# A pointwise convolution's weight folded into the lower half of an output projection, on one Trainium2 core

## The chip, the cores and the metric

The kernel runs on 1 core of one Trainium2 chip. The metric is the device time of one execution in microseconds (us), as the median of several runs. The engines are called as the profile calls them: PE is TensorE's matmul, PEld its weight load, DVE is VectorE, ACT is ScalarE, POOL is GpSimd, SP is SyncE, which here only issues DMAs. SPq and ACTq are the DMA queues of SP and ACT.

## What is computed

One decoder layer for 2048 tokens and a model width of 1024, in float32. Cut to what matters:

```python
def conformer_conv(u, conv_dw, conv_dw_b, conv_ln_g, conv_ln_b, w_conv_pw):
    a, gate = jnp.split(u, 2, axis=-1)
    h = a * jax.nn.sigmoid(gate)
    h = causal_depthwise_conv(h, conv_dw) + conv_dw_b          # 31 taps
    h = jax.nn.silu(layer_norm(h, conv_ln_g, conv_ln_b))
    return h @ w_conv_pw                                       # 512 x 512

...
        hn = rms_norm(h, mix_pre_g)
        proj = hn @ w_in                                       # 1024 x 1792
        attn_out = sliding_window_attention(q, k, v, attn_sinks, rel_bias)
        conv_out = conformer_conv(u, ...)
        mixed = jnp.concatenate([attn_out, conv_out], axis=-1) @ w_out   # 1024 x 1024
        h = h + rms_norm(mixed, mix_post_g)
        hn = rms_norm(h, ffn_pre_g)
        ff = (jax.nn.silu(hn @ w_gate) * (hn @ w_up)) @ w_down
        h = h + rms_norm(ff, ffn_post_g)
```

The convolution's part of the mixed output is swish(...) @ w_conv_pw @ w_out[512:1024]: two matrix products in a row with nothing between them.

## The kernel before

The 2048 tokens are worked in four tiles of 512 (NT = 4, T = 512), the 1024 channels in eight blocks of 128 (KC = 8). Float32 products are made from two parts: each operand is split into a rounded high part and the low rest, and `three` (L165) issues high x high, high x low and low x high into one PSUM bank. A split is one copy on ACT for the high part and one subtraction on POOL or DVE for the low part (`split_w`, L106, for weights). Low parts that are used again are kept in DRAM (`lo_in`, `lo_out`), so that later tiles load them.

The stages, by the letter that stands after @ in the profile's tile names (fc@C is a tile fc that stage C made; the names that the profile prints leave the tile's number out):

- A, t = 0 to 3: the input projection, 14 units of 24 matmuls of 128x128 by 512 columns each. Weights pass through `raw` (2 buffers) and `w` (6 buffers).
- B: sliding window attention in blocks of 128 tokens, with its bands and transposes in PSUM tiles tr.
- C: the convolution. `stage_taps` (L536) runs the 31 taps on DVE and keeps the result in DRAM (y_scr). `stage_tail` (L550) transposes it, takes the layer norm, transposes back, forms the swish in `conv_tail` (L565) and multiplies by w_conv_pw. That last part, per tile: four splits of the swish, then for each of four output blocks a load of a weight block (w_pw), a split, 4 x 3 = 12 matmuls into the PSUM tile ct, a copy z by ACT with a factor of one half, and a store to `mixT` on ACT's queue. So 48 matmuls in each of four tails.
- W, w = 0 to 3: the output projection (`stage_w`, L670). It loads the activations from mixT (blocks 0 to 3 attention, 4 to 7 convolution) and splits them, takes w_out in pairs of blocks and halves of the columns through `weight` (L117), and adds the partial sums on DVE. W0 splits the weights itself and stores the low parts to `lo_out`; W1 to W3 split the high part again and load the low part.
- H: transposes and operands for the feed-forward. F and G: its up and down products, in two halves of two tiles (0, 1 and 2, 3), by a scheme with seven instead of eight products.

What sets the order: one generator per stage yields between pieces of work with an estimate of the TensorE time that they take. `run` (L1309) drives a main generator (A, then W1, F, F, G, and again), and after each of its yields pumps the lanes: lists of side stages, each with a rate, the share of the main work's time that its own may use (class Lane, L1234). Tails C0 and C1 are in lane ld; C2, W2, C3, W3 follow each other in lane lw beside the first G. Taps are in lane lc, with a lower priority on DVE. W0 starts when the fourth projection tile has started and C0 is done (L1321). From these emissions a scheduler makes one fixed order for each engine; each engine and each DMA queue then works strictly in that order.

Buffers that are named below: wx has 1, mid 4, chl 5, mb 2, fc 3, w 6, raw 2, the PSUM banks mm 4, tr 3, ct 1.

## Time and profile before

| | us |
|---|---|
| median of 3 runs | 2050.37 |
| lowest and highest run | 2043.07, 2054.49 |
| span of the profiled execution | 2045.2 |

The page gives no other time for the profiled execution than its span, from the first to the last instruction. A row of a group reads: line, engine, operation, tile written <- tiles read, shapes, count | busy us, mean ns of one | idle time of the engine just before them and what ended it. A row of the timeline begins with its start and its length in us. A row of a stretch (window) gives for each engine its busy time and in brackets its count, then the clock granted to TensorE as a share of full speed, the DMA engines' busy share and GB/s. A row of waits reads: engine and line, what was waited for, us in total, how often, the longest. A DMA row gives the queue, the count, the size of one and the median us from issue to landing.

Where the stages lie in the span, by the first and last matmuls of the timeline: W0 and the fourth projection tile from about 338 to 487 us, W1 and the operands H to about 610, the first G from 1036 to 1393. The products of the four tails stand at 290.7 to 330, 497.6 to 536, 1120 to 1150 and in the stretch up to 1295.

### The profile page before, as it was taken

Reading aid. Unit: us, or ns where it says so; the run is one execution under the profiler, and the core shown is the slowest. Engines: PE = TensorE matmul, PEld = TensorE weight load, DVE = VectorE, ACT = ScalarE, POOL = GpSimd, SP = SyncE. Lnnn points to the kernel's source line nnn. Section 1 sums busy time; section 2 is a strip of 40 time slices with the busy share of each in tenths; the row PEclk is TensorE's granted clock in tenths of the full one; section 3 lists DMA queues with packets and bytes.
Section 4 is the critical chain, followed back from the end, with each engine's and each line's share of the span. In section 5 each row is a group of like instructions: output and inputs, shape, how many; then the busy total and the mean of one; then the engine's idle time right before and its main releaser. Section 6 shows DMA issues by size and latency. Waiting matters only on the chain. (4 is left out here: it accounts for less than half of the span.)

```text
span 2045.2 us, 27190 instructions
## 1 busy us (share of the span) xinstructions
PE 1959.9 (96%) x8826; PEld 1565.3 (77%) x8826; DVE 1499.2 (73%) x2623; ACT 984.4 (48%) x1938; POOL 408.5 (20%) x466
## 2 busy tenths in 40 slices
PE   8999999999989999999989999999999999999997
PEld 6777767776667778778878878877788888888886
DVE  4999896995885899887749985577666665545557
ACT  5355455456546633334346457556643433345443
POOL 4011223333111300000001012115423333221003
PEclk9999999999999999999999999999999999999998
DMA  8787645578559876884486778678954453366654
GB/s 305 256 300 228 205 135 185 180 235 279 186 155 330 292 242 224 294 270 168 140 262 205 231 260 287 191 278 304 337 177 162 149 169 112 103 236 212 206 190 144
DMA packets 235902, 451.44 MB, mean 221 GB/s; under 512 B 23496, under 2 KB 49264, under 8 KB 235760
## 3 DMA queue, kind: packets, MB, share of 16 engines
q1 hardware_dynamic: 215216, 419.30, 62.6%
q10 hardware_dynamic: 20544, 30.42, 4.0%
q8 instruction: 69, 1.13, 0.2%
q14 instruction: 73, 0.60, 0.1%
HBM read 330.60 MB, written 119.02 MB: 220 GB/s over the span
## 5 line engine op out<-in xcount | busy, mean ns | idle before, releaser
L85 DVE SCALAR_TENSOR_TENSOR fc@C<-glu@C,colt,fc@C 128x512 f32<-128x512 f32 x480 | 367.7, 778 | 3.5
L846 PE MATMUL mm@F<-hl@H,w@F 128*128 128x512 f32 x1056 | 253.3, 390 | 2.5 <-ACT mm@F L886 1.5
L1116 PE MATMUL mm@G<-hl@G,hl@G 128*128 128x512 f32 x924 | 230.0, 398 | 8.2 <-DVE x@G L85 4.8
L846 PEld LDWEIGHTS mm@F<-hl@H,w@F 128*128 128x128 f32 x1056 | 197.6, 188 | 44.7 <-ACT mm@F L886 2.3
L170 PE MATMUL mm@A<-hl@A,w@A 128*128 128x512 f32 x840 | 207.3, 398 | 5.2 <-ACT w@A L110 1.4
L1116 PEld LDWEIGHTS mm@G<-hl@G,hl@G 128*128 128x128 f32 x924 | 174.6, 191 | 47.0 <-ACT hl@G L759 6.9
L1116 PE MATMUL mm@G<-w@G,hl@G 128*128 128x512 f32 x876 | 199.4, 389 | 0.0
L759 ACT ACTIVATE w@F<-chl@F 128x512 fp32r<-128x512 f32 x220 | 134.8, 624 | 130.9 <-PE mm@F L846 122.2
L1116 PEld LDWEIGHTS mm@G<-w@G,hl@G 128*128 128x128 f32 x876 | 164.4, 188 | 34.1
L170 PEld LDWEIGHTS mm@A<-hl@A,w@A 128*128 128x128 f32 x840 | 155.9, 189 | 42.2 <-ACT w@A L110 2.2
L85 DVE TENSOR_TENSOR w@F<-chl@F,w@F 128x512 fp32r<-128x512 f32 x198 | 145.4, 738 | 33.8 <-ACT w@F L759 33.4
L846 PE MATMUL mm@F<-ql@H,w@F 128*128 128x512 f32 x528 | 127.9, 391 | 11.0 <-ACT w@F L759 7.3
L846 PE MATMUL mm@F<-mid@H,w@F 128*128 128x512 f32 x528 | 130.4, 392 | 2.8 <-ACT mm@F L886 2.6
L846 PE MATMUL mm@F<-p@H,w@F 128*128 128x512 f32 x528 | 130.6, 393 | 0.0
L846 PE MATMUL mm@F<-x@H,w@F 128*128 128x512 f32 x528 | 127.4, 395 | 2.3 <-ACT fa@F L908 2.3
L846 PEld LDWEIGHTS mm@F<-ql@H,w@F 128*128 128x128 f32 x528 | 98.6, 188 | 33.7 <-ACT w@F L759 8.1
L846 PEld LDWEIGHTS mm@F<-x@H,w@F 128*128 128x128 f32 x528 | 99.8, 190 | 24.0 <-ACT fa@F L908 2.8
L846 PEld LDWEIGHTS mm@F<-mid@H,w@F 128*128 128x128 f32 x528 | 98.3, 188 | 26.0 <-ACT mm@F L886 4.6
L846 PEld LDWEIGHTS mm@F<-p@H,w@F 128*128 128x128 f32 x528 | 100.1, 190 | 21.3 <-ACT at@F L1007 0.4
L170 PE MATMUL mm@W<-w@W,hl@W 128*128 128x512 f32 x384 | 102.3, 411 | 7.7 <-ACT hl@W L681 6.8
L110 ACT ACTIVATE w@A<-raw@A 128x512 fp32r<-128x512 f32 x110 | 67.6, 627 | 82.7 <-PE mm@A L170 50.8
L476 POOL TENSOR_SCALAR_AFFINE_SELECT p@B<-p@B 128x512 f32<-128x512 f32 x62 | 59.1, 959 | 228.0 <-ACT p@B L474 226.3
(301 smaller groups left out, 3422.8 us busy)
## 6 DMA issues: line engine op xcount, KB each, us to landing
mids<-fa@F SPq DMA_DIRECT2D x154, 256.0 KB, 2.8
raw@A<-w_in SPq DMA_DIRECT2D x55, 512.0 KB, 4.5
w@A<-lo_in SPq DMA_DIRECT2D x84, 256.0 KB, 3.5
fc@G<-mids SPq DMA_DIRECT2D x77, 256.0 KB, 3.5
fa@G<-mids SPq DMA_DIRECT2D x75, 256.0 KB, 4.3
gb@F<-keeps SPq DMA_DIRECT2D x72, 256.0 KB, 4.3
raw@W<-w_out SPq DMA_DIRECT2D x32, 512.0 KB, 5.1
w@W<-lo_out SPq DMA_DIRECT2D x48, 256.0 KB, 3.9
```

The lines of the kernel that those rows point to most:

```text
L85: r = op(*args, **kw)
L110: act(w[:, 0], raw, AF.Copy)
L170: mat(o, a, b, start=first and i == 0, stop=last and i == n - 1)
L476: nc.gpsimd.affine_select(out=pg[:, kb].rearrange("p (i q) -> p i q", q=P), in_=pg[:, 1].rearrange("p (i q) -> p i q", q=P), compare_op=AL ...
L759: act(w[:, 0], x, AF.Copy)
L846: mat(o, w[:, a, ks], op[k][:, b], start=first and n == 0, stop=n == 11, skip_group_check=not first)
L1116: mat(banks[b], p_, q_, start=start and z == 0, stop=stop and z == 2, skip_group_check=True)
```

## The change

w_conv_pw and the lower half of w_out are multiplied once, by a new stage U (`stage_fold`), to a 512 x 1024 matrix. It is split into high and low parts and kept in DRAM (`fold`). The convolution's tail stops at the swish and stores that to mixT, with the factor of one half moved into the constants lnh. W's lower half loads both parts from `fold` in one DMA of 512 KB per block and splits nothing there. The stores to mixT go through SP's queue instead of ACT's. w_conv_pw is passed to the kernel transposed.

```diff
-    lo_out = dr.tile([2, KC, P, T], F32, name="lo_out")
+    lo_out = dr.tile([2, KC // 2, P, T], F32, name="lo_out")
+    fold = dr.tile([2, 4, P, 2, T], F32, name="fold")
...
             v = f2("fc")
-            act(v, b, AF.Identity, scale=ln_g[:, c : c + 1], bias=ln_b[:, c : c + 1])
+            act(v, b, AF.Identity, scale=lnh[:, c : c + 1], bias=lnh[:, 4 + c : 5 + c])
             stt(v, th, 1.0, v, ALU.add, ALU.mult)
-            h = hl("chl")
-            act(h[:, 0], v, AF.Copy)
-            ptt(h[:, 1], v, h[:, 0].bitcast(F32), ALU.subtract)
-            sc.append(h)
-            yield 2
-            lab[0] = L
-        for m in range(4):
-            raw = f2("fc")
-            nc.sync.dma_start(raw, w_pw[m])
-            w = split_w(raw, "mb" if t == 1 and m % 2 else "chl").rearrange("p a (k c) -> p a k c", c=P)
-            o = ct()
-            three(o, [((w[:, 0, k], w[:, 1, k]), (sc[k][:, 0], sc[k][:, 1])) for k in range(4)])
-            z = f2("gb" if t > 1 else "fc")
-            act(z, o, AF.Copy, scale=0.5)
-            nc.scalar.dma_start(mixT[4 + m, :, t * T : (t + 1) * T], z)
-            yield 2
-            lab[0] = L
+            nc.sync.dma_start(mixT[4 + c, :, t * T : (t + 1) * T], v)
+            yield YZ
+            lab[0] = L
+
+    def stage_fold():
+        lab[0] = "U0"
+
+        def two(src):
+            raw = f4("wx", (P, 2, T))
+            nc.sync.dma_start(raw, src)
+            return raw
+
+        wp = []
+        for i in range(2):
+            lab[0] = "U0"
+            raw = two(w_pw[2 * i : 2 * i + 2].rearrange("c p t -> p c t"))
+            wp += [split_w(raw[:, j], "mid") for j in range(2)]
+            yield 2.76
+        for n in range(2):
+            wo = []
+            for i in range(2):
+                lab[0] = "U0"
+                c = 4 + 2 * i
+                raw = two(w_out[c : c + 2, :, n * T : (n + 1) * T].rearrange("c p t -> p c t"))
+                wo += [split_w(raw[:, j], "chl") for j in range(2)]
+                yield 0.1 if n else 2.76
+            for m in range(4):
+                lab[0] = "U0"
+                o = mm()
+                ms = slice(m * P, (m + 1) * P)
+                three(o, [((wp[j][:, 0, ms], wp[j][:, 1, ms]), (wo[j][:, 0], wo[j][:, 1])) for j in range(4)])
+                f = hl("chl" if m % 2 else "mb")
+                act(f[:, 0], o, AF.Copy)
+                vtt(f[:, 1], o, f[:, 0].bitcast(F32), ALU.subtract)
+                nc.sync.dma_start(fold[n, m], f.bitcast(F32))
+                yield 2.76
...
-                ws = weight(w_out[2 * gi : 2 * gi + 2, :, n * T : (n + 1) * T].rearrange("c p t -> p c t"),
-                            lo_out[n, 2 * gi : 2 * gi + 2], w > 0)
+                if G * gi < 4:
+                    ws = weight(w_out[2 * gi : 2 * gi + 2, :, n * T : (n + 1) * T].rearrange("c p t -> p c t"),
+                                lo_out[n, 2 * gi : 2 * gi + 2], w > 0)
+                else:
+                    ws = [hl("w") for _ in range(2)]
+                    for j in range(2):
+                        nc.sync.dma_start(ws[j].bitcast(F32), fold[n, 2 * gi - 4 + j])
...
+    YZ = 1.0
...
+    lu = Lane(0.6, 0)
...
-    lanes = [lb, lc, lw, ld, lf, lh, lt]
+    lanes = [lb, lc, lu, lw, ld, lf, lh, lt]
...
-    lw.add("W0", stage_w(0, True, 2, "x", "hl", "fa", mm), lambda: "A3" in started and "C0" in ld.done)
+    lu.add("U", stage_fold(), lambda: "A2" in started)
+    lw.add("W0", stage_w(0, True, 2, "x", "hl", "fa", mm), lambda: "A3" in started and "C0" in ld.done and "U" in lu.done)
...
-    wp = kblocks(f(w_conv_pw))
+    wp = f(w_conv_pw).T.reshape(4, P, 4 * P)
```

How the order moves, at three places. The names in the rows are tiles with their numbers; the numbers differ between the two programs.

PE in the third projection tile, before: one unit of the projection (its results mm@A_477) and the start of the next, with a transpose of the first tail (ct@C) and attention (tr@B) between.

```order
L170 MATMUL mm@A_477_2967<-hl@A_278_1812,w@A_475_2961 128x512 x3
L170 MATMUL mm@A_477_2967<-hl@A_279_1816,w@A_475_2961 128x512 x3
L170 MATMUL mm@A_477_2967<-hl@A_280_1820,w@A_475_2961 128x512 x3
L170 MATMUL mm@A_477_2967<-hl@A_281_1824,w@A_475_2961 128x512 x3
L584 MATMUL ct@C_344_2185<-ident,yt@C_303_1978 128x128 x4
L170 MATMUL mm@A_477_2967<-hl@A_289_1873,w@A_476_2964 128x512
L426 MATMUL tr@B_410_2532<-kz,ql@A_297_1922 128x256
L170 MATMUL mm@A_477_2967<-hl@A_289_1873,w@A_476_2964 128x512 x2
```

PE in the third projection tile, now, where the first product of the fold's second half stands (mm@U_480, from the weights chl@U of w_out and mid@U of w_conv_pw).

```order
L170 MATMUL mm@A_471_2928<-hl@A_292_1886,w@A_470_2925 128x512 x3
L170 MATMUL mm@U_480_2984<-chl@U_475_2970,mid@U_367_2302 128x512 x3
L170 MATMUL mm@U_480_2984<-chl@U_476_2973,mid@U_368_2305 128x512
L170 MATMUL mm@A_485_3009<-hl@A_278_1813,w@A_483_3003 128x512 x3
L170 MATMUL mm@A_485_3009<-hl@A_279_1817,w@A_483_3003 128x512 x2
L170 MATMUL mm@U_480_2984<-chl@U_476_2973,mid@U_368_2305 128x512 x2
L170 MATMUL mm@A_485_3009<-hl@A_279_1817,w@A_483_3003 128x512
L170 MATMUL mm@A_485_3009<-hl@A_280_1821,w@A_483_3003 128x512 x3
```

The fold's matmuls stand between the projection's, in the same engine order. The other half of this product (from chl@U_478 and chl@U_479) follows 24 rows further down, behind the rest of this projection unit and a piece of attention; all 96 of them stand before the fourth projection tile begins.

PE at the feed-forward's first operands (tr@H), before, with two products of the second tail (mb@C_644 and chl@C_648 are split weight blocks).

```order
L170 MATMUL ct@C_645_3902<-chl@C_613_3724,mb@C_644_3899 128x512 x3
L777 MATMUL tr@H_831_4985<-ident,fa@H_830_4983 128x128 x4
L777 MATMUL tr@H_836_5006<-ident,fa@H_835_5004 128x128 x4
L777 MATMUL tr@H_845_5045<-ident,fa@H_844_5043 128x128 x4
L777 MATMUL tr@H_857_5085<-ident,fa@H_856_5083 128x128 x4
L170 MATMUL ct@C_649_3923<-chl@C_584_3577,chl@C_648_3920 128x512 x2
L473 MATMUL tr@B_862_5106<-ident,p@B_802_4834 128x128 x4
L170 MATMUL ct@C_649_3923<-chl@C_584_3577,chl@C_648_3920 128x512
```

PE at the same place now.

```order
L801 MATMUL tr@H_821_4962<-ident,fa@H_820_4960 128x128 x4
L801 MATMUL tr@H_826_4983<-ident,fa@H_825_4981 128x128 x4
L801 MATMUL tr@H_835_5022<-ident,fa@H_834_5020 128x128 x4
L801 MATMUL tr@H_847_5062<-ident,fa@H_846_5060 128x128 x4
L474 MATMUL tr@B_852_5083<-ident,p@B_792_4811 128x128 x4
L474 MATMUL tr@B_855_5102<-ident,p@B_792_4811 128x128 x4
L801 MATMUL tr@H_857_5112<-ident,fa@H_856_5110 128x128 x4
L170 MATMUL mm@W_864_5140<-w@W_862_5134,hl@W_839_5035 128x512 x2
```

The transposes follow each other with nothing but attention's transposes between them.

SP's queue in the first down projection beside the third tail, before: loads of the weight block w_pw, of W2's activations at@W and of G's operands.

```order
L1096 DMA fa@G_1800_10599<-mids_4796 128x512
L598 DMA fc@C_1665_9859<-w_pw 128x512
L679 DMA at@W_1725_10169<-mixT 128x512
L1096 DMA fa@G_1806_10642<-mids_4796 128x512
L1100 DMA mb@G_1807_10644<-td 128x512 x2
L1096 DMA fa@G_1816_10694<-mids_4796 128x512
L679 DMA at@W_1727_10174<-mixT 128x512
```

SP's queue there now.

```order
L590 DMA mixT<-fc@C_1615_9631 128x512
L698 DMA at@W_1679_9949<-mixT 128x512
L1120 DMA fa@G_1712_10139<-mids_4773 128x512
L718 DMA w@W_1708_10115<-fold 128x1024
L590 DMA mixT<-fc@C_1618_9646 128x512
L718 DMA w@W_1709_10116<-fold 128x1024
L698 DMA at@W_1704_10105<-mixT 128x512
L1124 DMA mb@G_1713_10141<-w_down 128x512 x2
```

The tail's stores to mixT and W2's loads of folded weights stand among G's loads; the loads of w_pw are gone.

More of the change, by code (lines that the diff above doesn't have):

```diff
@@ L579, in conv_tail @@
             act(yt[:, s], yt[:, s], AF.Identity, scale=r[:, s : s + 1], bias=nmr[:, s : s + 1])
-        sc = []
         for c in range(4):
```

## The prediction

> **What bounds the kernel now.** I read the page's first two parts, then the table of stretches, then single rows of the timeline.
>
> ```profile
> span 2045.2 us, 27190 instructions
> PE 1959.9 (96%) x8826; PEld 1565.3 (77%) x8826; DVE 1499.2 (73%) x2623; ACT 984.4 (48%) x1938; POOL 408.5 (20%) x466
> ```
>
> TensorE is busy for 96% of the span and idle for 85.3 us (2045.2 - 1959.9). The next engine, VectorE, stands at 73%. So work taken from TensorE should show, if the stretch it leaves was full and stays full. The stretches say where that is so (columns: PE, PEld, DVE, ACT, POOL busy, each with its count, then clock, DMA share, GB/s):
>
> ```profile
> 190.00:270.00 80.00, 79.41 (x389) 58.69 (x388) 67.22 (x154) 41.03 (x105) 16.19 (x23) 1.00 0.65 198
> 455.00:545.00 90.00, 79.75 (x382) 56.84 (x381) 56.37 (x121) 56.15 (x120) 27.67 (x34) 0.96 0.70 236
> 1110.00:1205.00 95.00, 90.99 (x405) 74.02 (x404) 89.92 (x136) 44.05 (x78) 12.04 (x17) 1.00 0.72 226
> 1600.00:1650.00 50.00, 50.00 (x222) 41.42 (x221) 33.77 (x43) 20.14 (x36) 16.52 (x11) 1.00 0.50 170
> ```
>
> Row one is the third projection tile, where the fold will stand: PE has 0.6 us free. Row two holds the end of the projections, the second convolution tail and half of W1: PE is idle for 10.3 us, so some of it is a matter of latency. Row three is the third tail beside the first down projection: PE full, and DVE at 89.9 of 95. Row four gives the price of a matmul in a full stretch: 50.00 / 222 = 0.225 us for 128x128 by 512 columns. The 390 ns that the page gives for one is its passage, which overlaps the next.
>
> **The change part by part.** First the pointwise products that go.
>
> ```profile
> L170 PE MATMUL ct@C<-chl@C,chl@C 128*128 128x512 f32 x168 | 43.4, 394 | 0.4 <-ACT chl@C L110 0.4
> L170 PE MATMUL ct@C<-chl@C,mb@C 128*128 128x512 f32 x24 | 6.5, 406 | 0.0
> ```
>
> 168 + 24 = 192 matmuls, 48 in each of four tails. Their groups were busy 49.9 us, but a group's edges overlap its neighbours, so I take the full-stretch price: 192 x 0.225 = 43.2 us removed, 10.8 a tail. The fold adds 2 x 4 x 12 = 96 matmuls, 21.6 us, into the stretch with 0.6 us free. Net on PE: **-21.6 us**. W0 to W3 keep their number of matmuls. The order shows all fold products placed between the third tile's projections, so the first two tails (-21.6) pay for the fold (+21.6), and the gain is what the third and fourth save.
>
> Next, who takes part of it back. The second tail's products stand here now:
>
> ```profile
> 511.16 2.58 PE L170 MATMUL ct@C<-chl@C,mb@C 128*128 128x512 f32 x10
> 513.57 1.47 PE L777 MATMUL tr@H<-ident,fa@H 128*128 128x128 f32 x12
> 516.51 0.66 PE L777 MATMUL tr@H<-ident,fa@H 128*128 128x128 f32 x4 [1.46 <-ACT gb@H L797]
> 517.54 0.73 PE L170 MATMUL ct@C<-chl@C,chl@C 128*128 128x512 f32 x2 [0.38 <-ACT chl@C L110]
> 519.05 2.57 PE L170 MATMUL ct@C<-chl@C,chl@C 128*128 128x512 f32 x10
> 522.52 0.66 PE L473 MATMUL tr@B<-ident,p@B 128*128 128x128 f32 x4 [0.91 <-ACT gb@H L797]
> ```
>
> Two of the four products fill gaps in a chain of transposes (tr@H) that ScalarE paces by its copies (gb@H). Without the filler PE waits there. The other two products stand in full rows and are saved whole. The give-back lies between 0 (ScalarE loses the tail's copies there and speeds up) and 10.8 us (the whole stretch is paced by latency); two products are 24 x 0.225 = 5.4 us, less about 2.4 us for four ScalarE operations of 0.6 us that also go: 3.0, and 1 us more for new gaps. I take **+4**.
>
> A gap also slows what follows it:
>
> ```profile
> 337.83 7.36 PE L170 MATMUL mm@W<-w@W,hl@W 128*128 128x512 f32 x24 [3.98 <-ACT hl@W L681]
> 524.52 5.74 PE L170 MATMUL mm@W<-w@W,hl@W 128*128 128x512 f32 x24 [0.86 <-ACT hl@W L681]
> ```
>
> After a gap of 3.98 us the same 24 matmuls took 1.6 us more than after one of 0.86. Should the small gaps at the transposes join into one of about 4 us, this adds 1.6 to the +4, still inside its bounds. [...]
>
> The fold brings its operands through the tile wx, of which there is one buffer. Rows:
>
> ```profile
> wx@W<-x SPq DMA_DIRECT2D x4, 512.0 KB, 6.5
> L110 ACT ACTIVATE w@W<-raw@W 128x512 fp32r<-128x512 f32 x64 | 39.4, 627 | 20.6 <-PE mm@W L170 9.8 <-PE tr@W L170 4.3 <-issue 2.5
> L592 POOL TENSOR_TENSOR chl@C<-fc@C,chl@C 128x512 fp32r<-128x512 f32 x16 | 22.4, 1401 | 82.3 <-ACT chl@C L591 82.3
> L85 DVE TENSOR_TENSOR x@W<-x@W,mm@W 128x512 f32<-128x512 f32 x24 | 15.8, 676 | 0.0
> ...
> 287.88 1.94 PE L494 MATMUL tr@B<-p@B,vtok 128*64 128x512 f32 x8 [2.23 <-POOL p@B L476]
> 289.75 0.97 PE L426 MATMUL tr@B<-kz,ql@A 64*128 64x256 f32 x12
> ```
>
> One pass is a 512 KB landing (6.5), two ScalarE copies (1.25) and two GpSimd subtractions (2.8): 10.6 us. The first four passes go ahead of the products, beside projections. In the second half the last pair's load must wait until the pair before it is split; in the changed order one projection of 24 matmuls (5.4 us) and attention work like the last two rows (about 3 us) stand between a first and a last third of that product, against 6.5 + 0.63 + 1.4 = 8.5 us. Bounds: 0, or both passes of the second half (21.2) less that cover (8.4), 12.8. As the row counts come out nearly even, **+2**. The eight evacuations add 8 x 0.676 = 5.4 us to DVE, which has 12.8 us free in 190 to 270; if taps filled that, 5.4 would be lost, within the 12.8.
>
> The fourth term is VectorE under the third tail: 89.9 us of work in 95. With 10.8 us less of PE, 84.2 are left, so up to 89.9 - 84.2 = 5.7 us could be taken back, or nothing where the taps, which come last in order, slide on. I take **+2**.
>
> ScalarE and GpSimd lose work. ScalarE: 16 copies of the swish, 16 weight splits, 16 output copies and 32 splits of W's lower half (all about 0.6 us), against 20 new ones: 60 fewer, 37 us. GpSimd: 40 subtractions gone, 12 new, 39 us fewer. Neither sets the pace, so I cost this at nothing but for waits that they cause:
>
> ```profile
> PE tr@B L494 <- POOL p@B L476: 8.6, 4, 4.5
> PE mm@W L170 <- ACT hl@W L681: 6.8, 3, 4.0
> ```
>
> 15.4 us in all; bounds 0 and about -9 (the longest of both, 4.5 + 4.0, gone). Nearest are the waits beside the second tail: **-2**.
>
> Transfers: 64 issues go (16 of w_pw, 16 raw, 24 low parts, 8 stores of low parts), 62 come (6, 8 fold stores, 32 fold loads, 16 mixT stores, which leave the ScalarE queue). Bytes: 20 MB go, 23 come, of 451. W's lower weights now land as 512 KB instead of a 512 KB raw tile and 256 KB:
>
> ```profile
> raw@W<-w_out SPq DMA_DIRECT2D x32, 512.0 KB, 5.1
> w@W<-lo_out SPq DMA_DIRECT2D x48, 256.0 KB, 3.9
> fa@G<-mids SPq DMA_DIRECT2D x75, 256.0 KB, 4.3
> ```
>
> That is 5.1 instead of 3.9 after a buffer falls free, 1.2 us later, hidden behind the two pairs that the six w buffers hold ahead (24 matmuls, 5.74 us, a pair); without that cover 16 pairs a half would cost 16 x 1.2 = 19 us. I take 0.
>
> Sum: -21.6 + 4 + 2 + 2 - 2 = **-15.6 us**, a span of 2029.6. The median shown (2050.37) is 5.2 above the profiled span, inside the runs' 2043.07 to 2054.49, so I carry the difference over: 2050.4 - 15.6 = **2034.8 us**.
>
> **The rivals.**
>
> (a) The move to SP backfires: slower. Each mixT store now stands in SP's queue and waits there for VectorE's product; behind it in the third and fourth tail stand the loads fa@G, issued three steps ahead: 3 x 12 x 0.225 = 8.1 us, less 4.3 for landing, 3.8 us of slack. It decides once a store holds SP for over 3.8 us.
>
> ```profile
> SPq L1096 <- DVE hl@G L85: 130.1, 78, 7.0
> SPq L679 <- DMA mixT<-gb@C: 14.8, 8, 4.2
> SPq L114 <- POOL w@W L112: 42.5, 12, 8.9
> ```
>
> With the longest DVE hold, 7.0, at all eight stores: 8 x 3.2 = 25.6. In the projections the lead is two tiles of 24, 10.8 us, less about 5.1: 5.7 of slack, so eight mixT and eight fold stores cost 16 x 1.3 = 20.8. With -15.6 that is +30.8; with half the stores so unlucky, about 0. For it: SP is held by DVE 78 times already. Against: mean holds are 1.7 and 1.85 us, and eight stores that wait on POOL (3.5 on average) go. [...] I give it at three quarters of the price, 2050 + 20 = 2070.
>
> (b) Latency takes back both halves: the second tail's 10.8 whole and DVE's 5.7. -21.6 + 10.8 + 5.7 = -5.1, about 2045. For it: the 10.3 us idle of 455 to 545. Against: two of the four products stand in full rows, and taps can slide.
>
> (c) The relief counts in full: -21.6 - 9 = -30.6, about 2020, if ScalarE and GpSimd were what held W and attention. Against: neither row names an operation that goes; they wait for other work of these engines.
>
> **How the numbers follow.** About 0.5% (10 us) can be told from no change, so 2040.1 and 2060.6 are the borders. Forecast 0.55, its own range 2027 to 2043, of which 0.05 lies above 2040; (c) 0.16; (b) 0.18; (a) 0.11. Faster 0.50 + 0.16 = 0.66, same 0.05 + 0.18 = 0.23, slower 0.11. The range runs from 2020, the whole relief, to 2054, which holds (b) and the lower part of what (a) and the fold's 12.8 could do; about 0.06 is left below and 0.12 above.
>
> **What would show it.** Right: 96 fewer matmuls; the third projection tile about 21 us longer with PE still full; about 10 us shorter at the first tail and 5 to 8 at the second; the stretch from the first down projection to the second feed-forward about 18 us shorter. The ScalarE row ahead of tr@H should grow. Wrong: PE gaps before mm@U with wx as releaser (the fold's term); gaps before mm@G that end with a load of fa@G or mb@G (rival a); PE idle between 455 and 610 grown by 10 us (b). The prediction is wrong in kind if PE's busy time does not fall by about 21 us.

## The result, and the profile after

| kernel | runs | median, us | lowest to highest |
|---|---|---|---|
| before | 12 | 2048.5 | 2043.07 to 2054.49 |
| changed | 12 | 2049.64 | 2042.82 to 2057.31 |

The ratio of the times is 1.000, with a 95% interval of 0.9984 to 1.0017. A gain of 15.6 us (ratio 0.992) was forecast; nothing that can be measured came. The time lies inside the range of 2020 to 2054, the forecast of a clear gain does not hold.

The profiled execution of the changed kernel was its slowest run (2057.31 us). A second profile was therefore taken of both kernels on later chips, called "the change again" and "before again" below, at 2052.0 and 2053.7 us. The page's first lines, first of the changed kernel:

```profile
span 2055.5 us, 26866 instructions
PE 1955.9 (95%) x8730; PEld 1558.7 (76%) x8730; DVE 1498.2 (73%) x2631; ACT 952.5 (46%) x1878; POOL 366.6 (18%) x438
```

then of the change again:

```profile
span 2050.3 us, 26866 instructions
PE 1950.6 (95%) x8730; PEld 1555.7 (76%) x8730; DVE 1496.8 (73%) x2631; ACT 954.1 (47%) x1878; POOL 377.8 (18%) x438
```

and of before again:

```profile
span 2052.0 us, 27190 instructions
PE 1967.2 (96%) x8826; PEld 1571.3 (77%) x8826; DVE 1502.6 (73%) x2623; ACT 985.5 (48%) x1938; POOL 407.5 (20%) x466
```

The 96 matmuls are gone (8826 to 8730), ScalarE lost 31 us and GpSimd 30. But PE's busy time fell by 16.6 us (1967.2 - 1950.6), in the first pair of profiles by 4.0 (1959.9 - 1955.9), not by 21.6. In the second pair its idle time grew from 84.8 to 99.7 us. Busy time counts a matmul as long as it lasts, so it also holds the matmuls that a lower clock made longer: in the change again 24 matmuls mm@W behind the transposes tr@H took 7.86 us from 546.1 on, with a granted clock of 0.50 up to 550.6, and in the first profile of before 5.74 us at clock 1.00. Where, the table of stretches tells. Columns: PE, PEld, DVE, ACT, POOL busy, each with its count, then clock, DMA share, GB/s. The three rows run from the first matmul of the third projection tile to the first of W0; from the first of W1 to the first of the feed-forward part F; and from F's 400th matmul to its 1680th. Before again:

```profile
165.20:337.10 171.90, 164.77 (x814) 121.96 (x812) 141.12 (x299) 88.02 (x210) 44.41 (x49) 0.99 0.62 192
487.80:544.80 57.00, 53.15 (x261) 37.91 (x260) 31.97 (x92) 35.94 (x85) 9.63 (x9) 0.97 0.70 229
694.00:1005.30 311.30, 299.93 (x1286) 243.87 (x1286) 260.27 (x418) 114.00 (x205) 0.29 (x1) 0.98 0.72 234
```

The change again:

```profile
165.70:356.10 190.40, 179.23 (x875) 131.74 (x873) 166.50 (x341) 92.55 (x219) 54.92 (x53) 0.98 0.64 209
510.10:562.70 52.60, 41.15 (x202) 30.01 (x202) 38.16 (x102) 33.07 (x80) 3.62 (x4) 0.87 0.71 226
706.80:1025.60 318.80, 303.48 (x1285) 245.42 (x1285) 264.05 (x424) 117.75 (x211) 5.13 (x3) 0.97 0.69 230
```

The second stretch tells most. It lost 59 matmuls, the second tail's 48 products among them, some 12 us of work, and became only 4.4 us shorter: PE is now idle for 11.5 us of it instead of 3.9, and its clock fell from 0.97 to 0.87. The third stretch has the same work in both programs and took 7.5 us more, though F as a whole hardly got longer (more on this below).

To separate work from waiting, every matmul record was put beside its place in the program. A stretch's content is its matmuls, each at the median start-to-start interval of its form (0.227 us for 128x512 in the projections); its excess is its duration less its content, so it holds idle time, a slow clock, and what else stands on PE. Two profiles each, in us:

| stretch | excess before | excess of the change | content, before to change |
|---|---|---|---|
| third projection tile to W0 | 12.6, 13.1 | 20.5, 19.2 | +12.4 |
| W0 to W1 | 14.2, 16.1 | 22.2, 20.7 | -1.4 |
| W1 to F | 9.7, 9.9 | 17.3, 17.7 | -12.1 |
| F, first 400 | 20.0, 21.7 | 12.1, 15.3 | +1.2 |
| F, 400th to 1680th | 18.7, 20.2 | 30.9, 27.8 | 0 |
| to the end of the first G | 26.0, 28.7 | 34.1, 32.1 | -20.3 |
| all else | 16.1, 14.4 | 12.9, 11.7 | -1.5 |
| sum | 117.3, 124.1 | 150.0, 144.5 | -21.7 |

The content fell by the 21.6 us that were forecast. Over it, 20 us (124.1 to 144.5, the two runs near their medians) to 33 us of new waits appeared.

### The profile page after: what moved, and what is told of

The parts are those of the page before. It is cut to its first block, busy times and chain, and to the rows that moved or that the text cites. A ratio compares the mean times of both kernels' runs of the same rounds, so it can differ in the third digit from the quotient of the medians.

```text
span 2055.5 us, 26866 instructions
## 1 busy us (share of the span) xinstructions
PE 1955.9 (95%) x8730; PEld 1558.7 (76%) x8730; DVE 1498.2 (73%) x2631; ACT 952.5 (46%) x1878; POOL 366.6 (18%) x438
## 4 chain that ended last, share of the span: by engine, by line
PE 61%; DMA 16%; DVE 14%; issue 4%; ACT 4%; POOL 1%; SPq 0%; ACTq 0%; DVEq 0%; POOLq 0%
PE mm@F L870 25%; PE mm@G L1140 13%; PE mm@A L170 11%; DVE fc@C L85 4%; PE tr@W L170 4%; PE mm@W L170 3%; DMA chl@F<-w_gate 2%; DMA at@W<-mixT 2%; DMA gb@F<-keeps 2%; PE tr@B L427 1%; DVE w@F L85 1%; PE tr@B L495 1%; DMA mb@G<-w_down 1%; DVE hl@G L85 1%; DVE chl@F L85 1%
## 5 line engine op out<-in xcount | busy, mean ns | idle before, releaser
L1140 PE MATMUL mm@G<-hl@G,hl@G 128*128 128x512 f32 x924 | 228.3, 397 | 12.9 <-DVE hl@G L85 8.5
L170 PE MATMUL mm@A<-hl@A,w@A 128*128 128x512 f32 x840 | 213.9, 401 | 5.4 <-ACT w@A L110 3.1
L1140 PEld LDWEIGHTS mm@G<-w@G,hl@G 128*128 128x128 f32 x876 | 164.4, 188 | 34.1
L170 PE MATMUL tr@W<-w@W,ql@W 128*128 128x512 f32 x384 | 99.7, 400 | 5.7 <-ACT ql@W L700 5.4
```

Source lines behind the costliest of these rows:

```text
L170: mat(o, a, b, start=first and i == 0, stop=last and i == n - 1)
L1140: mat(banks[b], p_, q_, start=start and z == 0, stop=stop and z == 2, skip_group_check=True)
```

## The experiments

The theories that the expectations name. A: the fold costs its matmuls and as much again in stalls where it stands, and the removal comes back in full. B: the fold costs its matmuls; half of the removal is taken back, since the products had filled waits. C: the swish stores on SP's queue hold loads (rival (a)). D, formed later: the fold's excess lies in reading its finished halves. E: it lies where the fold is computed. F: the changed order lands the rest of the program in other waits, either way. G: the fold's operand splits hold GpSimd's queue and the attention behind them.

**A second profile of the change.** No edit.

> The changed kernel once more, for a second profile beside runs of before on the same chip. All theories: 2044 to 2055, ratio to before 0.997 to 1.003; the profile tells which of the waits in the first 650 us of the earlier profile (5.40 us at the start of the first output projection, 3.42 in the fourth projection tile, 4.09 at the first transposes of the feed-forward part) come back in place and which were of that one execution.

Measured: 2052.32 us (11 runs), ratio to before 1.0009 (0.9995 to 1.0023). All three waits came back in their places, with 3.18, 4.49 and 4.21 us.

**No fold.** The fold's lane and the lower half's loads go:

```diff
-    lu.add("U", stage_fold(), lambda: "A2" in started)
...
-                if G * gi < 4:
-                    ws = weight(...)
-                else:
-                    ws = [hl("w") for _ in range(2)]
-                    for j in range(2):
-                        nc.sync.dma_start(ws[j].bitcast(F32), fold[n, 2 * gi - 4 + j])
+                ws = weight(...)
```

> Left out: the pointwise weight (neither product nor fold); the conv tail stops at the swish as in the change, and the output projection's lower half reads the plain weight with the first kernel's own split. TensorE content: 192 matmuls (43.2 us) less than before. Theory A (the fold costs its own 21.6 us and as much again in stalls, and the removed products come back in full): about 2005, ratio 0.978 to 0.982. Theory B (the fold costs its 21.6 us, but half of the removed products' time is not given back, since they filled waits): about 2027, ratio 0.988 to 0.991. Theory C (stores of the swish on SP's queue hold back loads, the fold is cheap): 2020 to 2027 with SP's holds unchanged, so this run tells A from the others, and the next one C from B.

Measured: 2014.42 us (4 runs), ratio 0.9821 (0.9801 to 0.9841). So the removal alone brings 37.8 us (2052.25 - 2014.42, with before's median of the same session) of its 43.2, and the fold costs 37.9 (2052.32 - 2014.42) where its matmuls are 21.6. The prediction's terms make 39.2 of the removal (43.2 - 4 - 2 + 2) and 23.6 of the fold (21.6 + 2). In total time the fold's half is the one that is off. The time is below B's 2027 and above A's 2005.

**Stores on ScalarE's queue.**

```diff
-            nc.sync.dma_start(mixT[4 + c, ...], v)
+            nc.scalar.dma_start(mixT[4 + c, ...], v)
```

> The change with one edit: the 16 swish stores are issued on ScalarE's queue, where the first kernel issued its pointwise stores, instead of SP's. Theory C (these stores hold SP's queue and loads behind them): 2030 to 2038, ratio about 0.993. Theories A and B: 2046 to 2053, same as the change, ratio 0.999 to 1.002; ScalarE might wait for the swish's last product instead (a few us at the four tails).

Measured: 2057.28 us (11 runs), ratio 1.0029 (1.0018 to 1.004): 5 us slower than the change beside it. In the changed kernel the stores did hold SP, by the table of SP's waits (us in total, times, longest):

```profile
SPq L590 <- DVE fc@C L85: 30.2, 12, 5.0
```

but to take these 30 us out of SP's queue gained nothing. And in neither profile of the change does a wait of PE before mm@G end with a load, which was the sign of rival (a): all end with VectorE's hl@G. Theory C and rival (a) are out as the cause. The 5 us by which this run is slower were expected by no theory, and their cause was not looked for.

**Every product of the fold twice.**

```diff
-            for m in range(4):
+            for m in (0, 0, 1, 1, 2, 2, 3, 3):
...
-                yield 2.76
+                yield 1.38
```

> The change with every one of the fold's eight products computed twice (96 matmuls more, 21.6 us), with its copies and stores, in the same stretch. Theory A (a fold costs twice its matmuls): about 2085 to 2095, ratio 1.017 to 1.022. Theories B and C (a fold costs its matmuls): about 2071, ratio 1.010 to 1.012. Well below 2071 would mean that the matmuls of the fold fill waits.

Measured: 2067.9 us (4 runs), ratio 1.008 (1.0063 to 1.0097). The second copy cost 15.6 us, less than its matmuls' 21.6, while the first cost 37.9. So a fold does not cost twice its matmuls by itself, and theory A falls. By stretch: from the third projection tile to W0 this kernel took 215.0 us, 23 to 25 more than the change, which is the second copy's own matmuls and little else. F's 400th to 1680th matmul took 311.3 us, 7 to 11 less than in the change.

**Fold computed, plain weight read.** The lower half is read as in the run without a fold, the fold stays.

> The fold is computed and stored exactly as in the change, but the output projection's lower half reads the plain weight and splits it, as the first kernel did (so the pointwise weight is missing from the output). The two runs before put the whole fold at about 38 us (2014 without it, 2052 with it), 21.6 of them its matmuls. Theory D (the rest lies in reading the finished halves: 16 loads of 512 KB in place of raw weight and low half): 2036 to 2042, with the third and fourth output projections as long as in the run without a fold (338 us for the first down-projection part). Theory E (the rest lies where the fold is computed): 2050 to 2054. Theory F (the rest is drift further on, in the feed-forward part, which a changed order meets in another phase): anything from 2040 to 2054, with the difference inside the feed-forward part.

Measured: 2048.08 us (12 runs), ratio 0.9992 (0.9978 to 1.0007), against 2049.64 and 2052.32 of the change: if the order made no difference, 1.6 to 4.2 us would lie in reading the halves. Theory D falls (2036 to 2042), and E's range (2050 to 2054) is missed too, by 2 us; F's holds the time.

**A third of the fold's matmuls.**

```diff
-                three(o, [((wp[j][:, 0, ms], wp[j][:, 1, ms]), (wo[j][:, 0], wo[j][:, 1])) for j in range(4)])
+                for j in range(4):
+                    mat(o, wp[j][:, 0, ms], wo[j][:, 0], start=j == 0, stop=j == 3)
```

> The change with 4 matmuls for each of the fold's products in place of 12: only the high halves are multiplied (left out: both low parts, 64 matmuls of 96, 14.4 us; the output is less exact). All loads, splits, copies and stores of the fold stay. If the fold's matmuls cost their time and the rest of the 38 us is loads, splits, copies and where they fall: 2052 - 14 = 2038. If the matmuls cost more than their time, because they stretch the stretch in which the third projection waits: 2028 to 2034. If they cost less, because others of the fold's steps set its pace: 2044 to 2052.

Measured: 2016.8 us (5 runs), ratio 0.9839 (0.9817 to 0.986): 64 matmuls less, 14.4 us, took 33 to 36 us away, and loads, splits, copies and stores of the fold, with the 32 matmuls left, cost next to nothing (0 to 2.4 us over the two runs without a fold). That was expected by none of the three cases. Some 10 us of it lie far from the fold: F's 400th to 1680th matmul took 309.8 us here.

**The fold later, spread out.** Its weight halves go into buffers that are free after the first tail, and it starts there. The lines shown are not all of it: W0 starts without the fold and only its lower half waits for it, the second tail waits until the fold is done, and the fold's results pass through the fc buffers, with two stores of 256 KB instead of one of 512.

```diff
-    lu = Lane(0.6, 0)
+    lu = Lane(0.45, 0)
...
-    lu.add("U", stage_fold(), lambda: "A2" in started)
+    lu.add("U", stage_fold(), lambda: "C0" in ld.done)
```

> The change with the fold moved later: its weight halves in buffers that are free after the first conv tail, its products spread from the end of the third projection tile to the start of the first output projection, where the trace shows TensorE waiting. If waits there are latency that other matmuls can fill: 2042 to 2047 (the excess between the start of the third projection tile and the first output projection, 20 us over the matmul content in the change, falls to about 12). If they are not: 2050 to 2056.

> The same with the fold at a lower rate, so that its products lie among the first half of the first output projection too, up to the point where its lower half needs them. If the waits can be filled: 2040 to 2046, lower than or equal to the run before. If they cannot, or if the fold's copies and stores now hold back that projection: 2052 to 2060.

Measured: 2075.31 us (5 runs), ratio 1.0118 (1.0101 to 1.0135), and 2083.91 us (4 runs), 1.0163 (1.0143 to 1.0183). A clear miss. The stretch from the third tile to W0 at rate 0.45, and two of PE's waits in it:

```profile
167.20:386.80 219.60, 189.08 (x874) 134.87 (x873) 192.65 (x377) 91.48 (x216) 55.99 (x53) 0.93 0.55 176
```

```profile
PE tr@B L495 <- POOL p@B L477: 9.6, 5, 5.3
PE mm@U L170 <- ACT chl@U L110: 5.6, 1, 5.6
```

The same work (874 matmuls against 875) took 29 us more than in the change, with PE idle for 30.5 us. The time did not fall as it should have if the moved fold filled waits: PE waited 5.6 us for an operand's split, 9.6 in the attention for GpSimd's masks and 5.4 for ScalarE in the first tail, ahead of the fold. How much of the 29 us comes from the later place, and how much from the held tail, the other buffers and the order, was not separated.

**Rates 0.8 and 0.5 of the fold's lane.** One number; all operations stay.

```diff
-    lu = Lane(0.6, 0)
+    lu = Lane(0.8, 0)
```

> The change with the fold's lane at rate 0.8 in place of 0.6: the same work, in the same projection tile, a little denser; only the order of instructions differs. Theory F (a changed order lands the later parts in another phase of waits, worth up to 8 us either way): 2040 to 2060, with the difference from the change inside the first feed-forward part. Theory E (the fold's price sits where it is computed): 2048 to 2056, the first feed-forward part (mm@F0, 494 to 502 us from first to last matmul so far) as long as in the change.

> The same with rate 0.5, a little more spread. Theory F: 2040 to 2060, not the same as the run at 0.8. Theory E: 2046 to 2054, if anything a little less than the change, since fewer of the attention's instructions wait behind the fold's.

Measured: 2041.85 us (12 runs), ratio 0.9957 (0.9944 to 0.997), and 2058.56 us (10 runs), 1.0044 (1.0028 to 1.006). The same work in the same tile, in another order, is 16.7 us apart, which theory E does not allow and F does, though not inside F alone as was expected: from 400th to 1680th matmul F's excess is 22.7 at 0.8 and 24.1 at 0.5, so the rest lies ahead of it. At 0.5 PE waited 3.7 us inside the fold, for VectorE, and 5.8 us for a mask. The stretch from W1 to F, with the work of the change, took 64.60 us at clock 0.74 (change again: 52.60 at 0.87; at 0.8: 47.50 at 0.86, with 11 matmuls fewer in it):

```profile
512.70:577.30 64.60, 52.88 (x206) 36.07 (x206) 38.78 (x103) 34.12 (x81) 3.62 (x4) 0.74 0.59 193
```

**Two thirds of the fold's matmuls.**

> The change with 8 matmuls for each of the fold's products (left out: the product of the pointwise weight's low part; 32 of 96 matmuls, 7.2 us; the output is less exact). So far: 0 matmuls 2014, 32 matmuls 2017, 96 matmuls 2052, 192 matmuls 2068. If each matmul costs its 0.225 us over a fixed part and the rest is scatter of the order: between 2024 and 2044. If there is a step between a third and the whole, where the fold begins to set the pace of its tile: 2017 to 2026 or 2045 to 2050.

Measured: 2033.4 us (6 runs), ratio 0.9926 (0.9906 to 0.9945). With 0, 32, 64, 96 and 192 matmuls the medians are 2014 to 2017, 2017, 2033, 2050 to 2052 and 2068: steps of about 1, 16, 18 and 16, where the matmuls alone make 7.2, 7.2, 7.2 and 21.6. From 32 to 96 matmuls that is over twice their price. Over the whole, from 0 to 192, it comes to 52 us for 43.2. F tells part of why the steps are so uneven: its 400th to 1680th matmul took 309.8, 312.3, 318.8 to 321.9 and 311.3 us with 32, 64, 96 and 192 matmuls in the fold, so it is longest in the change and does not grow with the fold's work. The rest may be the order too; a step at which the fold begins to set its tile's pace is not excluded.

**No fold, again.**

> The run without a fold once more (left out again: the pointwise weight), since 4 times are few for the main comparison, and for a second profile: 2012 to 2020, ratio 0.980 to 0.984. If the first feed-forward part is again 495 us and not the change's 502, that difference belongs to the kernels and not to single executions.

Measured: 2016.86 us (4 runs), ratio 0.9841 (0.982 to 0.9863). F's 400th to 1680th matmul took 309.5 and 310.5 us in the two profiles without a fold, 309.7 and 311.2 in those of before, and 321.9 and 318.8 in those of the change. So that difference belongs to the program, although nothing of the change stands there. F as a whole, from first to last matmul, took 494.9 and 496.2 us without a fold and 502.4 and 502.1 in the change, as expected; but it took 499.2 and 502.9 before. The stretch from W1 to F, in the profile of this second run, has the change's gaps without a fold:

```profile
483.90:533.80 49.90, 42.17 (x207) 30.59 (x206) 38.53 (x103) 31.50 (x78) 3.62 (x4) 0.86 0.70 238
```

PE is idle for 7.7 us at clock 0.86, where the first kernel has 3.9 at 0.97: that loss is there without the fold, so it comes with the removal.

**The low halves of the fold's operands on VectorE.** With and without the rate of 0.8, and a rate of 1.0 by itself. The positions that these expectations name count from the trace's start, 11 us ahead of the span's: their 231 is 220 in the rows.

```diff
-            wp += [split_w(raw[:, j], "mid") for j in range(2)]
+            wp += [split_w(raw[:, j], "mid", on_pool=False) for j in range(2)]
...
-                wo += [split_w(raw[:, j], "chl") for j in range(2)]
+                wo += [split_w(raw[:, j], "chl", on_pool=False) for j in range(2)]
```

> The change with the low halves of the fold's eight operand splits made on VectorE in place of GpSimd, so that the attention's masks on GpSimd stand behind none of them; all else, the rate 0.6 too. In the repeated profile of the change ScalarE waited 10.9 us for a fold operand, GpSimd's low halves behind it, the masks behind these, and TensorE 6.4 us for a mask at 231 us. Theory G (that hold is a cause of the fold's excess): the wait at 231 us is gone and the time is 2040 to 2047. Theory F (the order as a whole decides, whichever wait comes first): 2036 to 2060, and the wait there is replaced by one of VectorE's or ScalarE's nearby.

> The same edit with the fold's lane at rate 0.8, which alone gave 2042. Theory G: 2034 to 2040. Theory F: 2036 to 2056, with no fixed relation to the run with the one edit.

> The change with the fold's lane at rate 1.0. If denser is better in itself (2059 at 0.5, 2052 at 0.6, 2042 at 0.8): 2034 to 2042. If it is the accident of an order: 2036 to 2060 with no trend.

Measured: 2039.78 us (6 runs), ratio 0.9939 (0.9926 to 0.9952); with rate 0.8, 2045.18 us (12 runs), 0.9967 (0.9955 to 0.998); rate 1.0 alone, 2045.14 us (12 runs), 0.9971 (0.9956 to 0.9986). The first is the fastest version that does all of the work, 0.6% ahead of the first kernel. What it took away can be followed row by row. The change again, timeline of GpSimd, SP, PE and ScalarE (start, duration, and in brackets the idle time before and what ended it):

```profile
206.67 9.28 POOL L112 TENSOR_TENSOR chl@U<-wx@U,chl@U 128x512 fp32r<-128x512 f32 x2 [5.82 <-ACT chl@U L110]
215.91 4.20 POOL L477 TENSOR_SCALAR_AFFINE_SELECT p@B<-p@B 128x512 f32<-128x512 f32 x4
...
215.97 0.38 SPq L599 DMA_DIRECT2D wx@U<-w_out  x1
...
220.16 3.27 PE L495 MATMUL tr@B<-p@B,vtok 128*64 128x512 f32 x8 [6.39 <-POOL p@B L477]
...
220.59 1.15 ACT L110 ACTIVATE chl@U<-wx@U 128x512 fp32r<-128x512 f32 x2 [10.94 <-DMA wx@U<-w_out]
```

GpSimd worked 9.28 us on two low halves, 7.6 of them on the first. The four attention masks stand behind them in its queue, so PE waited 6.39 us for a mask. The one buffer of wx came free only at 215.9, so SP could not issue the next operand's load earlier and ScalarE waited for it 10.94 us. With the low halves on VectorE, GpSimd and PE:

```profile
204.66 4.72 POOL L477 TENSOR_SCALAR_AFFINE_SELECT p@B<-p@B 128x512 f32<-128x512 f32 x4 [8.68 <-ACT p@B L475]
...
211.19 1.94 PE L495 MATMUL tr@B<-p@B,vtok 128*64 128x512 f32 x8
```

The masks are done at 209.4 and PE does not wait.

The first profile of the change has the hold in another form. There no low half took over 1.75 us, the masks were in time, and PE waited a little later, for VectorE:

```profile
228.53 1.86 PE L427 MATMUL tr@B<-kz,ql@A 64*128 64x256 f32 x12 [3.96 <-DVE sm@B L437]
```

VectorE's taps were slower there: from 204.9 us they took 1.07 us each (14 in 14.99 us), beside four low halves of GpSimd (3.04 and 3.20 us a pair), while in the second profile, beside the long low half, they took 0.67 each (13 in 8.70). Of the ten profiles with the fold in this place and its low halves on GpSimd, five have a long low half and a wait for a mask of 5.8 to 6.4 us, the other five no long one and a wait for sm@B of 2.8 to 4.0. In the two profiles with the low halves on VectorE neither wait stands there. The excess of the stretch from the third tile to W0 falls from 19.2 and 20.5 to 11.4 us, and at rate 0.8 from 17.3 to 12.1: for this stretch it is shown that the low halves on GpSimd cost time, though the hold of the masks, which theory G names, is only one of two ways. These are single profiles, and the one of 11.4 is that of the fastest run (2034.28 us). Yet from W1 to F the excess then rises from 17.3 and 17.7 to 23.8, and at 0.8 from 13.5 to 27.1, so the two edits together gain nothing over either alone: 2045.18 us is 5 us slower than the low halves alone, and against the rate alone the intervals of the ratios overlap. Theory G's 2034 to 2040 is missed here. The row of that stretch for the low halves on VectorE:

```profile
491.00:550.20 59.20, 45.05 (x206) 32.00 (x206) 40.05 (x105) 34.95 (x81) 5.76 (x8) 0.80 0.68 220
```

So G's edit works where the fold stands, and F holds for the whole. Rate 1.0 is not faster than 0.8 (the intervals overlap), as a trend with the rate would have it; a trend that levels off at 0.8 is not excluded by four rates.

**The first kernel again.**

> The first kernel again, for a second profile: a time of 2045 to 2055. It tells which of its stretches vary between executions: the first profile was 2047, at the lower end of its times. All theories: 36 us of waits over the matmul content between the third projection tile and the first matmul of the feed-forward part, and 499 us for the first feed-forward part, each within 4.

Measured: 2052.53 us (8 runs), ratio 1.0 (0.9988 to 1.0013). F took 502.9 us from first to last matmul, 3.7 more than in the first profile, and the 36.5 us of excess ahead of F became 39.1 (13.1 + 16.1 + 9.9): both within the 4.

## Why the prediction missed, step by step

**The content was right.** -21.6 us of matmuls were forecast; the records hold -21.7. That PE's busy time fell by less, which the prediction called wrong in kind, does not speak against the count: that time also grew by slow matmuls (the 24 of 7.86 us alone make 2.1). VectorE under the third tail was near: to the end of the first G the kernel without a fold has 27.3 and 31.2 us of excess against 26.0 and 28.7, +1.9 where +2 was taken (the change has +5.8). The relief was put beside the second tail, where the waits grew; that "all else" fell by 3.0 us, near its -2, is luck as far as the runs show. One sum of the prediction is wrong without effect: in rival (a) half the stores come to 23.2 - 15.6 = +7.6 us, not to about 0.

**The give-back of the removal was sized at half.** The prediction took +4, at the second tail's transposes alone, and let the first tail's 10.8 us count whole. By the profiles without a fold the excess rises by 4.1 us from the third tile to W0, 3.9 to W1 and 5.1 to F, and 3.5 come back in F's first 400: 9.6 us in all. At the place that was named it is dearer than the prediction had it. In PE's timeline of the change again:

```profile
533.24 0.66 PE L801 MATMUL tr@H<-ident,fa@H 128*128 128x128 f32 x4 [0.23 <-ACT gb@H L821]
538.10 2.82 PE L801 MATMUL tr@H<-ident,fa@H 128*128 128x128 f32 x12 [4.21 <-ACT gb@H L821]
...
543.40 1.11 PE L474 MATMUL tr@B<-ident,p@B 128*128 128x128 f32 x4 [1.62 <-ACT gb@H L821]
...
546.08 7.86 PE L170 MATMUL mm@W<-w@W,hl@W 128*128 128x512 f32 x24
```

The small gaps did join into one, of 4.21 us. After it 12 transposes took 2.82 us, where the prediction's row had 1.47, and 24 matmuls 7.86 where it had 5.74: another 3.5 us, not 1.6. Two more gaps, of 1.62 and 0.52 us, ended at 543.4 and 545.0 us, and the granted clock was 0.50 from 536.9 to 550.6 us, for 13.65 us (in the first profile of the change the gap was 4.09 us, and the clock 0.50 from 540.6 to 554.0). The clock's column for the whole stretch, 0.97 before and 0.87 now, sums it up. The 1.6 us that the prediction read off two rows, each behind one gap, are too few here, where three gaps lie beside 13.65 us at the lower clock. The prediction also took it that ScalarE's copies set the pace. In the row ahead of the 4.21 us gap ScalarE itself waited 3.13 us, for a store of an earlier gb@H to land (hT<-gb@H), as it already had before the change (1.54 and 1.33 us), so losing the tail's copies could not speed it up there.

**The fold's operands were looked for in the wrong place.** The prediction took +2 for loads through the one wx buffer, and said that gaps before mm@U would show it wrong. There were none in the two profiles of the change. The splits held SP, ScalarE (10.94 us) and above all GpSimd (9.28), or VectorE was slower beside GpSimd's (1.07 us a tap against 0.67), and the gap opened before an attention matmul that waited for one of these two. The term counted what waits for the operand, and not what is queued behind those who split it or runs beside them. It is worth 5 to 9 us in its stretch (19.2 and 20.5 to 11.4; 17.3 to 12.1), inside the bounds of 0 to 12.8. Transfers at 0 held within 4 us, by the run that read the plain weight.

**The step that failed** is the sum itself: "the first two tails (-21.6) pay for the fold (+21.6), and the gain is what the third and fourth save". It prices each place that the edit touches and takes the rest as unchanged. By the means of two profiles, from the first matmul of the third projection tile to the first of F, where tails and fold cancel to about 1 us of content, the kernel became 20 us longer (378.2 to 398.1), where the terms put there come to +4 (give-back 4, operand loads 2, relief -2). F as a whole became 1 us longer. All else became 16.8 us shorter, where 21.6 - 2 = 19.6 was forecast. That makes 16 us more ahead of F, 1 in F and 3 elsewhere: 20 in all, the forecast's 15.6 and the 4.3 us by which the two pairs of profiles differ (2048.6 to 2052.9; the medians differ by 0.1 and 1.1).

Ahead of F the excess rose by 7 us before W0, 6 between W0 and W1 and 8 from there to F. With the low halves on VectorE the first 7 are gone, though 4 of them stand in the kernel without a fold too, which has no such halves. Of the last 8 us 5 stand without a fold, by the transposes. For the 6 between, in a stretch that the edit hardly touches, no experiment names a cause: in the change again PE waited there 4.5 us for fa@A and 2.6 for x@W, both from ScalarE, and without a fold 4.7 us in the second tail for ScalarE and 3.1 for a load instead. In the prediction's terms: ahead of F the removal gave back 13 us where +4 was taken, and the fold brought 8 of excess where +2 was.

Inside F the excess moved: the first 400 matmuls became 5.9 us shorter, the next 1280, which the edit doesn't touch and the prediction doesn't name, 9.9 longer, the last ones 2.9 shorter. At rates 0.5, 0.8 and 1.0 F took 495.4 to 496.6 us, 6 less than in the change.

The order that the scheduler makes for the whole program differs as far as F, and the waits with it. PE's waits of over 0.5 us between F's 400th and last matmul end at these matmuls of F, counted from its first:

| kernel | F's matmuls at which a wait ends |
|---|---|
| the change, common to both profiles | 481, 552, 970, 1091, 1272, 1356 |
| no fold, again | 420, 540, 554, 588, 672, 948, 996, 1248, 1272 |
| the change at rate 0.8 | 420, 468, 588, 672, 948, 996, 1248, 1272 |

The places return in the same program. At rate 0.8 seven of the eight are those of the kernel without a fold, so there the fold left F nearly as it was. What PE waited for in that stretch, change again:

```profile
PE mm@F L870 <- DVE gb@F L85: 8.7, 5, 3.6
PE mm@F L870 <- DVE fa@F L85: 4.2, 3, 2.8
PE mm@F L870 <- ACT w@F L783: 2.2, 1, 2.2
```

Without a fold VectorE's gb@F costs 2.1 us there, and ScalarE's mm@F 6.2. Why VectorE's part is late in one program and not in the other was not settled; that the order alone can move the time by 16.7 us is shown by the rates.

**Of the rivals**, (b) named the right place, and its 10.8 us of give-back is near the 9.6 found, though over three stretches; its second half was wrong: not VectorE under the third tail but the fold's stretch and the one behind it took the rest. Its 2045 us lies nearest to the measured time, in part by luck. (a) fell with the stores on ScalarE's queue and the missing waits for loads, (c) with the small relief.

How far off the fold's price was depends on the order as much as on the fold: over the kernels without one (2014.42 and 2016.86 us) it cost 35.5 to 37.9 us in the change, 25.0 to 27.4 at rate 0.8 and 22.9 to 25.4 with its low halves on VectorE, where 23.6 had been forecast.

## What to carry to other kernels

In a kernel that is 96% bound by one engine, the work taken away can be counted to a tenth of a microsecond, but the time also contains some 120 us of short waits, and any edit that re-deals the order re-deals these: here 16.7 us for one constant. Before believing or dropping an edit of under 1%, run it under two or three orders that mean the same. Where filler goes, look at what it covered: the wait that opens can cost more than its length, as here the 4.21 us, which came with a granted clock of 0.50 for 13.65 us. And where an operand is loaded and split, list everything that stands behind these instructions, on each queue, and what runs beside them, before pricing the load.

## What the runs showed of the hardware

One GpSimd subtraction of 128x512, at the same place of the program, took 1.3 to 1.6 us in some profiles and about 7 in others. The tile's view has all eight of its kind (minimum, median, maximum in ns); first the changed kernel, then the change again:

```profile
L112 POOL TENSOR_TENSOR chl@U<-wx@U,chl@U x8: 1273/1727/1747, 207.4 to 292.1; 128x512 fp32r<-128x512 f32 x8
```

```profile
L112 POOL TENSOR_TENSOR chl@U<-wx@U,chl@U x8: 1268/1714/7614, 206.7 to 292.3; 128x512 fp32r<-128x512 f32 x8
```

Of the ten profiles with the fold in the third projection tile and its low halves on GpSimd, five have one such instruction (6.5 to 7.7 us), always near 206 to 207 us, and five none (1.84 us at most). Beside each long one, 10 to 12 operations of VectorE took their usual time (0.77 us on average); beside the subtraction at that place in the other profiles VectorE's were slower (1.26). So at this place of the ten profiles one of the two engines took longer, GpSimd (6.5 us or more for the one subtraction) or VectorE (1.26 us for an operation instead of 0.77); what decides which is open. And some 206 matmuls of the stretch from W1 to F took 49.9 us (no fold again, clock 0.86), 52.6 (0.87), 59.2 (0.80) or 64.6 (0.74). PE was idle for 7.7, 11.5, 14.2 and 11.7 us of it, so the gaps alone do not explain the differences: PE was busy for 42.2, 41.2, 45.1 and 52.9 us with nearly the same matmuls (202 to 207), longest in the two rows with the lowest clock, 0.80 and 0.74.
